# The dense layer's second pass: the gate row is formed in the first pass, and the scaled residual is added tile by tile

## The chip, the core and the metric

One core of a Trainium2 chip runs the whole program. Its engines each work through their own list of instructions in order: TensorE (PE in the profile; PEld are its weight loads), VectorE (DVE), ScalarE (ACT), GpSimd (POOL), and SyncE (SP), whose list here is a queue of transfers (SPq). The engines wait for each other by semaphores. The metric is the device time of one execution in microseconds. Before the change three runs gave 3324.81, 3330.18 and 3332.77 us; the median is 3330.18 us.

## The reference

The kernel computes a trunk of two layers on a sequence of 1024 tokens with 1024 channels. Each layer has a token mixer and a channel mixer; the channel mixer of layer 0 is a dense SwiGLU with 2816 hidden channels, that of layer 1 a mixture of eight experts. The change touches the dense one:

```python
def _dense_swiglu(u, w_gate, w_up, w_down):
    h = jax.nn.silu(jnp.einsum("bsd,df->bsf", u, w_gate)) * jnp.einsum("bsd,df->bsf", u, w_up)
    return jnp.einsum("bsf,fd->bsd", h, w_down)
...
    u = x * (1.0 + sc2) + sh2
    ff = _dense_swiglu(u, ffn_w_gate[j], ffn_w_up[j], ffn_w_down[j])
    x = _layernorm(DEEPNORM_ALPHA * x + (1.0 + g2) * ff, ln2_g[layer], ln2_b[layer])
```

`g2` is a row of 1024 numbers that comes from the conditioning vector. `x` in the last line is the output of the mixer's layer norm, so that `DEEPNORM_ALPHA * x` is a normalized tile times a scaled row of gains plus a scaled row of biases.

## The kernel before

Matrix products are made of three products in a reduced fp32 type: each operand is split into a high part (ScalarE, L352) and a low part (VectorE or GpSimd, L353), and `mm3` (L356 to L360) multiplies high by high, high by low and low by high into one PSUM bank of 128x512.

The dense layer has two passes. `dense_up` goes over eleven pairs of hidden tiles; for each pair it loads 256 columns of both up-projections, makes seven block products of each, and writes the pair's activation `h` to a DRAM buffer `hd` (L970). After each pair a hook issues some of the loads and VectorE work of the conditioning vector.

`dense_down` goes over the 22 hidden tiles in groups of two (nine groups) and four (the last). For a group it loads the activations `hf` from `hd` (L991) and splits them into `hh` (ScalarE) and `hl` (VectorE); it loads the down weights of two tiles in one transfer of 1 MB, `fd` (L997), multiplies them by the gate row `G` on GpSimd (L999), and splits them into `fdw..h` (ScalarE) and `fdw..l` (VectorE). Then, for each of eight token tiles and both halves of the 1024 output columns, it makes one PSUM bank: two hidden tiles times three products are six matmuls of 128x512. A group of two tiles so has 16 banks and 96 matmuls. VectorE adds each bank to the tile's running sum `xres` in SBUF (L1016). Six PSUM banks are in turn for this; a seventh bank can be started when the first has been added.

The running sums start as the residual: in group 0, before the first bank of a token tile, `residual` (L980 to L984) loads the normalized tile from DRAM and scales it in place with `gain` (L828 to L835): times the gain row `ln_g`, plus the bias row `ln_b`, the left half of the columns on GpSimd and the right half on VectorE. The two rows are loaded by `rows` (L815 to L826) and scaled on GpSimd (L824).

The gate row `G` is formed by `gate_row` (L325 to L337), which `dense_down` calls first (L977): for each of eight blocks VectorE makes a diagonal tile `dg` (L334), TensorE multiplies it by a tile of ones into a PSUM bank `gr` (L335), and VectorE adds one (L336).

The order on each engine isn't the order of the code: a scheduler places the instructions of the whole program by their dependences, by free buffers and by its own model of times. The buffers that matter here: two for the raw weights `fd`, six for the split weights `fdw`, 32 tiles of 128x1024 for `hf`, `hh`, `hl` and `xres`, six PSUM banks for `fd`.

Of the kernel before, what the change touches and what calls it, by code (L numbers as in the profile page):

```python
# [6 lines left out]
F32 = mybir.dt.float32  # L7
# [3 lines left out]
AF = mybir.ActivationFunctionType  # L11
OP = mybir.AluOpType
# [3 lines left out]
P = 128  # L16
D = 1024
# [50 lines left out]
class Trunk:  # L68
# [766 lines left out]
                eng.tensor_tensor(x[:, sl], x[:, sl], rows[i][:, sl], op=op)  # L835


    def dense_up(self, first, second, blocks, hook=lambda i: None):

# [114 lines left out]
        for fp in range(NF // 2):  # L956
            h = [self.s4([P, S], F32, f"h{2 * fp + j}") for j in range(2)]
            ms = [Matrix(fp, up, h) for up in range(2)]
            rest = (1, 6, 2, 7, 5, 4, 3)
            if fp == 0:  # L960
                for p in (1, 2):
                    for m in ms:
                        m.product(p)
                sums()
                rest = (6, 7, 5, 4, 3)
            for m in ms:
                for p in rest:
                    m.product(p)
            for j in range(2):
                nc.sync.dma_start(hd[(2 * fp + j) * P:(2 * fp + j + 1) * P, :], h[j])  # L970
            hook(fp)
        return hd

    def dense_down(self, l, hd, res_dram, rows, done, hook=lambda i: None):
        nc, w = self.nc, self.w
        dv = w["ffn_w_down"][0].rearrange("(f p) n -> p f n", p=P)
        G = self.gate_row(l, 5)  # L977
        xres = []

        def residual(t):  # L980
            x = self.s4([P, D], F32, f"xres{t}")
            nc.sync.dma_start(x, res_dram[t * P:(t + 1) * P, :])
            self.gain(x, rows, True)
            xres.append(x)  # L984
        groups = [2] * 9 + [4]
        f0 = 0
        for gi, gn in enumerate(groups):
# [16 lines left out]
                        self.split(*wd[-1], draw[:, j])  # L1004
            last = gi == len(groups) - 1
            for t in range(NT):
                if gi == 0:
                    residual(t)
                for dh in range(2):
                    ps = self.bank(f"fd{gi}{t}{dh}")  # L1010
                    for j in range(gn):
                        hk = [hs[j][x][:, t * P:(t + 1) * P] for x in range(2)]
                        self.mm3(ps, hk, [wd[j][x][:, dh * 512:(dh + 1) * 512] for x in range(2)],
                                 j == 0, j == gn - 1)
                    xs = xres[t][:, dh * 512:(dh + 1) * 512]
                    nc.vector.tensor_tensor(xs, xs, ps, op=OP.add)  # L1016
                if last:
                    self.normalize(xres[t], f"d{t}")
                    if t % 2 == 1:
                        done((t - 1, t), xres[t - 1:t + 1])  # L1020
            f0 += gn
            hook(gi)

    def residual_halves(self, pool, src, dst):
# [448 lines left out]
    def residual(self, xn, dst):  # L1473

        rows = self.rows(1, 1, pool=self.s4)

        def f(t):
            x = self.s4([P, D], F32, f"rx{t}")
            sl = slice(t * P, (t + 1) * P)
            self.nc.sync.dma_start(x, xn[sl, :])  # L1480
            self.gain(x, rows)
            self.nc.gpsimd.dma_start(dst[sl, :], x)
        return f
# [106 lines left out]
def build(tc, out, **w):  # L1590
    nc = tc.nc
    with ExitStack() as es:
# [5 lines left out]
        def ada_hook(n):  # L1598
            def f(*a):
                for _ in range(n):  # L1600
                    if todo:
                        T.ada_dve(*todo.pop(0))
            return f
# [29 lines left out]
            for t, x in zip(ts, tiles):  # L1633
                nc.sync.dma_start(st2["xr"][t * P:(t + 1) * P, :], x)
        T.results_init()
        hd = T.dense_up(*plain, blocks, lambda i: ada_hook(1 + i % 2)())
        T.dense_down(0, hd, xr, T.rows(0, 1, pool=lambda s, d, n: T.ln(n)), done2, ada_hook(1))
        npool.close()
        ada_hook(24)()
        T.ada_stack.close()  # L1640
# [42 lines left out]
```

## Time and profile before

| what | value |
|---|---|
| median of three runs | 3330.18 us |
| the profiled execution | 3329.88 us |
| its span | 3328.2 us |
| mean granted TensorE clock | 0.975 |
| PE busy | 3194.7 us, 96% |
| DVE busy | 2033.9 us, 61% |
| ACT busy | 1288.3 us, 39% |
| POOL busy | 706.2 us, 21% |
| second pass, group 0 begins | 927.68 us |
| group 1 begins | 982.73 us |
| group 2 begins | 1004.49 us |

The span is the profiled execution on the core; some 1.7 us of the measured time lie around it. Busy times are of the engine's own instructions. PE is near its limit over the program, so that what matters is where it isn't: its idle stretches, and stretches at the lower granted clock. The clock is given as a share of full speed: 1.00 is 2.4 GHz, 0.50 is 1.2 GHz, and a number between them is a mean over a stretch that has both.

### The profile page before, as it was taken

What the parts mean: (1) busy time and instruction counts of PE and PEld (TensorE: products, weight loads), DVE (VectorE), ACT (ScalarE), POOL (GpSimd) and SP (SyncE); (2) the same over time, 40 slices, a digit from 0 to 9 for tenths busy, and PEclk for the clock granted to TensorE, in tenths of its full rate; (3) what the DMA queues carried; (4) which work ended last, traced back from release to release, by engine and by line L of the source; (5) the groups of instructions that cost most, each with busy time, mean ns of one, the idle gap of its engine ahead of it and who ended that gap; (6) DMA issues with size and microseconds to landing.
All of it is one profiled execution on the core that took longest, in us unless ns stands there. A gap on an engine that the chain in (4) does not pass through costs nothing. (4 is left out here: it accounts for less than half of the span.)

```text
span 3328.2 us, 47451 instructions
## 1 busy us (share of the span) xinstructions
PE 3194.7 (96%) x18688; PEld 2841.8 (85%) x18688; DVE 2033.9 (61%) x2983; ACT 1288.3 (39%) x1991; POOL 706.2 (21%) x501
## 2 busy tenths in 40 slices
PE   8999988999969999999889999999999999999988
PEld 7878776888858889888789999999999998888876
DVE  6898887444487563455444366454554546666797
ACT  4322233333312143222143444444444455555563
POOL 2000108666672214101100042000000000000152
PEclk8999998999979999999889999999999999999998
DMA  8545631222243133121155476555655656566885
GB/s 249 161 150 162 233 115 64 84 94 76 97 178 106 46 128 98 55 84 57 46 177 158 152 237 227 175 176 167 196 189 185 192 176 204 190 202 209 272 284 181
DMA packets 429334, 518.48 MB, mean 156 GB/s; under 512 B 20969, under 2 KB 372461, under 8 KB 429104
## 3 DMA queue, kind: packets, MB, share of 16 engines
q1 hardware_dynamic: 414968, 468.32, 43.7%
q0 software_dynamic: 13840, 46.95, 3.9%
q8 instruction: 149, 2.44, 0.3%
q14 instruction: 81, 0.66, 0.1%
q10 hardware_dynamic: 296, 0.10, 0.0%
HBM read 459.37 MB, written 56.17 MB: 155 GB/s over the span
## 5 line engine op out<-in xcount | busy, mean ns | idle before, releaser
L1016 DVE TENSOR_TENSOR xres<-xres,fd 128x512 f32<-128x512 f32 x160 | 105.1, 684 | 68.1 <-PE fd L360 67.7
L1271 POOL DMA_INDIRECT xg<-xn,ixc x21 | 25.8, 1229 | 539.4 <-DVE ixc L1265 239.4
L307 DVE SCALAR_TENSOR_TENSOR acc<-ag,cond,acc 128x256 f32<-128x256 f32 x240 | 110.8, 506 | 40.1 <-DMA ag<-in_ada_w_dram 39.6
L927 DVE TENSOR_TENSOR fxu<-fu,fxu 128x512 f32<-128x512 f32 x77 | 52.2, 689 | 99.0 <-PE fu L360 98.9
L927 DVE TENSOR_TENSOR fxg<-fg,fxg 128x512 f32<-128x512 f32 x77 | 52.1, 689 | 97.7 <-PE fg L360 97.2
L1348 DVE TENSOR_TENSOR es<-es,eu 128x328 f32<-128x328 f32 (+4 forms) x110 | 49.1, 446 | 87.5 <-PE eu L360 86.0
L1416 POOL DMA_DIRECT2D ys<-yr x15 | 8.6, 573 | 439.5 <-ACT yr L1413 435.6
L999 POOL TENSOR_TENSOR fd<-fd,G 128x1024 f32<-128x1024 f32 x22 | 55.3, 2537 | 136.3 <-DMA fd<-in_ffn_w_down_dram 85.3
L952 POOL TENSOR_TENSOR h<-h,fxu 128x512 f32<-128x512 f32 x44 | 72.5, 1656 | 20.9 <-DVE fxu L927 20.5
L360 PE MATMUL L0mix<-L0woh,L0yl 128*128 128x512 f32 x128 | 51.1, 399 | 3.4 <-DVE L0yl L353 3.4
L358 PE MATMUL L0mix<-L0woh,L0yh 128*128 128x512 f32 x128 | 51.4, 402 | 1.7 <-ACT L0yh L352 1.5
L358 PE MATMUL L1mix<-L1woh,L1yh 128*128 128x512 f32 x128 | 52.7, 412 | 0.0
L359 PE MATMUL L0mix<-L0wol,L0yh 128*128 128x512 f32 x128 | 50.7, 396 | 1.5 <-DVE L0wol L353 1.5
L359 PE MATMUL L1mix<-L1wol,L1yh 128*128 128x512 f32 x128 | 52.0, 406 | 0.0
L360 PE MATMUL L1mix<-L1woh,L1yl 128*128 128x512 f32 x128 | 52.0, 406 | 0.0
L1291 PE MATMUL xt<-cst,xg 128*128 128x128 f32 (+2 forms) x168 | 30.9, 276 | 21.7 <-DMA xg<-xn,ixc 21.0
L1291 PEld LDWEIGHTS xt<-cst,xg 128*128 128x128 f32 (+2 forms) x168 | 22.5, 146 | 29.2 <-ACT ew001h L352 18.5
L352 ACT ACTIVATE hh<-hf 128x1024 fp32r<-128x1024 f32 x22 | 22.8, 1055 | 55.4 <-DMA hf<-hd 46.0
L1293 ACT ACTIVATE xu<-xt,B,A 128x256 f32<-128x256 f32 (+5 forms) x64 | 34.8, 572 | 21.2 <-PE xt L1291 18.5
L1347 ACT ACTIVATE es<-eg 128x328 f32<-128x328 f32 (+4 forms) x110 | 42.5, 387 | 0.0
L708 DVE RECIPROCAL L1rs<-L1rs 128x512 f32<-128x512 f32 x8 | 26.8, 3353 | 24.9 <-ACT L1rs L707 24.9
L504 POOL MEMSET L0z<- 128x2 f32 x4 | 0.5, 123 | 189.8 <-DVE L0yt L522 189.8
(6385 smaller groups left out, 12663.5 us busy)
## 6 DMA issues: line engine op xcount, KB each, us to landing
er<-in_moe_w_gate_dram SPq DMA_DIRECT2D x86, 1024.0 KB
er<-in_moe_w_up_dram SPq DMA_DIRECT2D x86, 1024.0 KB
dr<-in_moe_w_down_dram SPq DMA_DIRECT2D x70, 1024.0 KB
ag<-in_ada_w_dram SPq DMA_DIRECT2D x160, 256.0 KB
dr<-in_moe_w_down_dram SPq DMA_DIRECT2D x20, 768.0 KB
fg<-in_ffn_w_gate_dram SPq DMA_DIRECT2D x11, 1024.0 KB
fu<-in_ffn_w_up_dram SPq DMA_DIRECT2D x11, 1024.0 KB
hd<-h SPq DMA_DIRECT2D x22, 512.0 KB
```

The source lines that it names most:

```text
L307: V.scalar_tensor_tensor(acc, raw[:, kk], c, acc, op0=OP.mult, op1=OP.add)
L358: mm(out, a[0], b[0], start=start, stop=False)
L359: mm(out, a[0], b[1], start=False, stop=False)
L360: mm(out, a[1], b[0], start=False, stop=stop)
L927: add = lambda out, t: V.tensor_tensor(out, ps, t, op=OP.add)
L952: Q.tensor_tensor(d, d, c, op=OP.mult)
L999: nc.gpsimd.tensor_tensor(draw[:, j], draw[:, j], G, op=OP.mult)
L1016: nc.vector.tensor_tensor(xs, xs, ps, op=OP.add)
L1291: nc.tensor.transpose(ps[:, c * P:c * P + n], t[:n, k * P:(k + 1) * P], self.ident[:n, :n])
L1293: nc.scalar.activation(u, ps[:, :N], AF.Identity, bias=B[:, k:k + 1], scale=A[:, k:k + 1])
L1347: nc.scalar.activation(sg, pss[0][:, :N], AF.Silu)
L1348: nc.vector.tensor_tensor(sg, sg, pss[1][:, :N], op=OP.mult)
```

## The change

The call of `gate_row` moves from the start of `dense_down` to `dense_up`, after the seventh pair (`fp == 6`), inside `issue_after(put.ins)`, which queues those instructions of its block that are on the engine of the named one (here SP's queue, for the pair's last put) behind it; the instructions of `gate_row` are on VectorE and TensorE. The running sums get their buffers ahead of the groups. In group 0 they are not added to but written: ScalarE copies each PSUM bank to `xres`. The residual of token tile `gi` is loaded to another tile `xr` and scaled after group `gi`, over the whole width on GpSimd, and VectorE adds it to `xres` in one instruction of 128x1024.

```diff
-    def dense_up(self, first, second, blocks, hook=lambda i: None):
+    def dense_up(self, l, first, second, blocks, hook=lambda i: None):
...
             for j in range(2):
-                nc.sync.dma_start(hd[(2 * fp + j) * P:(2 * fp + j + 1) * P, :], h[j])
+                put = nc.sync.dma_start(hd[(2 * fp + j) * P:(2 * fp + j + 1) * P, :], h[j])
+            if fp == 6:
+                with self.tc.issue_after(put.ins):
+                    G = self.gate_row(l, 5)
             hook(fp)
-        return hd
-
-    def dense_down(self, l, hd, res_dram, rows, done, hook=lambda i: None):
+        return hd, G
+
+    def dense_down(self, l, hd, G, res_dram, rows, done, hook=lambda i: None):
...
-        G = self.gate_row(l, 5)
-        xres = []
+        xres = [self.s4([P, D], F32, f"xres{t}") for t in range(NT)]
 
         def residual(t):
-            x = self.s4([P, D], F32, f"xres{t}")
+            x = self.s4([P, D], F32, f"xr{t}")
             nc.sync.dma_start(x, res_dram[t * P:(t + 1) * P, :])
-            self.gain(x, rows, True)
-            xres.append(x)
+            self.gain(x, rows)
+            nc.vector.tensor_tensor(xres[t], xres[t], x, op=OP.add)
...
             for t in range(NT):
-                if gi == 0:
-                    residual(t)
                 for dh in range(2):
...
                     xs = xres[t][:, dh * 512:(dh + 1) * 512]
-                    nc.vector.tensor_tensor(xs, xs, ps, op=OP.add)
+                    if gi == 0:
+                        nc.scalar.activation(xs, ps, AF.Copy)
+                    else:
+                        nc.vector.tensor_tensor(xs, xs, ps, op=OP.add)
...
             f0 += gn
+            if gi < NT:
+                residual(gi)
             hook(gi)
```

The following rows are pieces of the engines' lists in both kernels (line, operation, output<-inputs, shape; the number behind a name is the buffer's).

TensorE, where the gate row's products stand. The tiles `u23tp` are the last transposes ahead of the dense layer, `gr` is the gate row's bank, `fg06`, `fg07` and `fg05` are products 6, 7 and 5 of the first pair. Before:

```order
L397 MATMUL u23tp3_3692<-cst_84,L0r7_3529 128x128
L335 MATMUL gr050_7185<-dg050_7186,cst_84 128x128
L335 MATMUL gr050_7185<-dg051_7189,cst_84 128x128
L335 MATMUL gr050_7185<-dg052_7192,cst_84 128x128
L335 MATMUL gr050_7185<-dg053_7195,cst_84 128x128
L335 MATMUL gr051_7199<-dg054_7200,cst_84 128x128
L335 MATMUL gr051_7199<-dg055_7203,cst_84 128x128
L358 MATMUL fg06_3893<-S2h0_3813,wg0T2_3890 128x512
L359 MATMUL fg06_3893<-S2l0_3814,wg0T2_3890 128x512
L358 MATMUL fg07_3910<-S3h0_3836,wg0T3_3907 128x512
L359 MATMUL fg07_3910<-S3l0_3837,wg0T3_3907 128x512
L335 MATMUL gr051_7199<-dg056_7206,cst_84 128x128
```

and now:

```order
L397 MATMUL u23tp3_3692<-cst_84,L0r7_3529 128x128
L335 MATMUL gr050_5923<-dg050_5924,cst_84 128x128
L335 MATMUL gr050_5923<-dg051_5927,cst_84 128x128
L335 MATMUL gr050_5923<-dg052_5930,cst_84 128x128
L335 MATMUL gr050_5923<-dg053_5933,cst_84 128x128
L335 MATMUL gr051_5937<-dg054_5938,cst_84 128x128
L335 MATMUL gr051_5937<-dg055_5941,cst_84 128x128
L358 MATMUL fg06_3893<-S2h0_3813,wg0T2_3890 128x512
L359 MATMUL fg06_3893<-S2l0_3814,wg0T2_3890 128x512
L358 MATMUL fg07_3910<-S3h0_3836,wg0T3_3907 128x512
L359 MATMUL fg07_3910<-S3l0_3837,wg0T3_3907 128x512
L335 MATMUL gr051_5937<-dg056_5944,cst_84 128x128
```

The rows are the same but for the buffers' numbers: all eight products of the gate row stand at the first pair in both lists. The diagonal tiles on VectorE stand at the same places in both lists too.

ScalarE in the second pass. `hh2` to `hh9` are the activations of hidden tiles 2 to 9, `fdw2h` the weights of tile 2, and `xres` is written by the copies of group 0, of which there are sixteen. Before:

```order
L352 ACTIVATE fdw1h_7233<-fd0_7225 128x1024
L352 ACTIVATE hh2_7436<-hf2_7435 128x1024
L352 ACTIVATE hh3_7442<-hf3_7441 128x1024
L352 ACTIVATE hh4_7609<-hf4_7608 128x1024
L352 ACTIVATE fdw2h_7450<-fd2_7447 128x1024
L352 ACTIVATE hh5_7615<-hf5_7614 128x1024
L352 ACTIVATE hh6_7782<-hf6_7781 128x1024
L352 ACTIVATE hh7_7788<-hf7_7787 128x1024
L352 ACTIVATE hh8_7965<-hf8_7964 128x1024
L352 ACTIVATE fdw3h_7455<-fd2_7447 128x1024
L352 ACTIVATE fdw4h_7623<-fd4_7620 128x1024
L352 ACTIVATE hh9_7971<-hf9_7970 128x1024
```

and now, from the last four copies:

```order
L1017 ACTIVATE xres6_7219<-fd061_7349 128x512
L1017 ACTIVATE xres7_7220<-fd070_7357 128x512
L352 ACTIVATE fdw3h_7420<-fd2_7412 128x1024
L1017 ACTIVATE xres7_7220<-fd071_7365 128x512
L352 ACTIVATE fdw4h_7593<-fd4_7590 128x1024
L352 ACTIVATE hh2_7401<-hf2_7400 128x1024
L352 ACTIVATE hh3_7407<-hf3_7406 128x1024
L352 ACTIVATE hh4_7579<-hf4_7578 128x1024
L352 ACTIVATE hh5_7585<-hf5_7584 128x1024
L352 ACTIVATE hh6_7757<-hf6_7756 128x1024
```

`fdw2h` now stands ahead of all sixteen copies, `fdw3h` ahead of the last of them, and `hh2` to `hh7` behind them; before, `hh2`, `hh3`, `hh4` stood ahead of `fdw2h` and `hh5` to `hh8` ahead of `fdw3h`.

SyncE's list of transfers in the second pass. `fd2`, `fd4`, `fd6` are the raw weights of groups 1, 2 and 3, `hf` the activations, `hd<-h20` and `hd<-h21` the last two activations on their way to DRAM. Before:

```order
L997 DMA fd4_7620<-in_ffn_w_down_dram 128x2x1024
L970 DMA hd_3729<-h20_6875 128x1024
L991 DMA hf3_7441<-hd_3729 128x1024
L970 DMA hd_3729<-h21_6876 128x1024
L991 DMA hf4_7608<-hd_3729 128x1024
L991 DMA hf5_7614<-hd_3729 128x1024
L991 DMA hf6_7781<-hd_3729 128x1024
L991 DMA hf7_7787<-hd_3729 128x1024
L991 DMA hf8_7964<-hd_3729 128x1024
L991 DMA hf9_7970<-hd_3729 128x1024
L991 DMA hf10_8138<-hd_3729 128x1024
L997 DMA fd6_7793<-in_ffn_w_down_dram 128x2x1024
```

and now:

```order
L993 DMA hf1_7227<-hd_3729 128x1024
L999 DMA fd2_7412<-in_ffn_w_down_dram 128x2x1024
L822 DMA ln1_g0_7207<-in_ln1_g_dram 128x1024
L822 DMA ln1_b0_7210<-in_ln1_b_dram 128x1024
L999 DMA fd4_7590<-in_ffn_w_down_dram 128x2x1024
L970 DMA hd_3729<-h20_6904 128x1024
L970 DMA hd_3729<-h21_6905 128x1024
L984 DMA xr0_7373<-xr0_2972 128x1024
L993 DMA hf2_7400<-hd_3729 128x1024
L999 DMA fd6_7768<-in_ffn_w_down_dram 128x2x1024
L993 DMA hf3_7406<-hd_3729 128x1024
L984 DMA xr1_7552<-xr0_2972 128x1024
```

The eight loads of the residual no longer stand ahead of `hf2` and `fd2`; one load of `xr` stands in each group. `fd2` now follows `hf1`, `hf2` has moved behind the last two activations, and `hf3` stands behind `fd6`, which it preceded by nine transfers.

On GpSimd the sixteen half-width operations of `gain` (L835) become sixteen of 128x1024; the product of `fd2` and `G` stands ahead of the scaling of the two rows; `xr0` stands behind the product of `fd4` and `G`, `xr1`, `xr2`, `xr3` behind that of `fd6`, and so on in pairs. On VectorE the sixteen operations of `gain` and the sixteen adds of group 0 are gone, and the eight adds of `xr` (L986 of the new code) stand one in each of groups 1 to 8, that of `xr0` ahead of group 1's first bank, that of `xr1` behind its seventh. TensorE's order in group 0 is the same; in group 1 the first six banks get their products with tile 2 first, and then those with tile 3.

## Rows read from the trace of the kernel before

**Rows 1.** The windows of the span around the second pass's first groups: start and end of the stretch, its length, then busy time (and instructions) of PE, PEld, DVE, ACT and POOL, the granted clock, the share of DMA, GB/s.

```profile
920.00:930.00 10.00, 10.00 (x46) 8.29 (x45) 5.40 (x7) 0.84 (x1) 6.20 (x3) 1.00 1.02 401
930.00:940.00 10.00, 6.00 (x27) 4.64 (x25) 10.00 (x9) 2.12 (x2) 10.00 (x7) 0.96 1.02 381
940.00:950.00 10.00, 0.00 (x0) 0.00 (x0) 10.00 (x7) 1.06 (x1) 10.00 (x7) 0.50 0.46 186
950.00:960.00 10.00, 2.71 (x6) 2.16 (x7) 9.95 (x7) 4.84 (x5) 10.00 (x5) 0.50 0.00 0
960.00:970.00 10.00, 7.36 (x25) 5.28 (x23) 9.67 (x6) 0.00 (x0) 10.00 (x5) 0.84 0.14 53
970.00:980.00 10.00, 8.44 (x20) 6.15 (x20) 6.04 (x8) 0.00 (x0) 4.75 (x4) 0.50 0.17 54
1000.00:1200.00 200.00, 200.00 (x898) 165.46 (x897) 133.70 (x196) 39.57 (x54) 35.26 (x17) 1.00 0.22 76
```

**Rows 2.** The timeline of PE from the start of group 0 (first row) to the starts of groups 1, 2 and 3 (last three rows): start, length as modelled, engine, line, operation, output<-inputs, and in brackets the idle time before it and what ended it.

```profile
927.68 0.39 PE L358 MATMUL fd<-fdw0h,hh 128*128 128x512 f32 x1
...
935.61 0.39 PE L360 MATMUL fd<-fdw1h,hl 128*128 128x512 f32 x1
957.29 0.80 PE L358 MATMUL fd<-fdw0h,hh 128*128 128x512 f32 x1 [21.29 <-DVE xres L1016]
...
972.25 0.63 PE L358 MATMUL fd<-fdw1h,hh 128*128 128x512 f32 x1
972.68 0.63 PE L359 MATMUL fd<-fdw1l,hh 128*128 128x512 f32 x1
...
982.73 0.39 PE L358 MATMUL fd<-fdw2h,hh 128*128 128x512 f32 x1
...
1004.49 0.39 PE L358 MATMUL fd<-fdw4h,hh 128*128 128x512 f32 x1
...
1026.25 0.39 PE L358 MATMUL fd<-fdw6h,hh 128*128 128x512 f32 x1
```

**Rows 3.** The groups of instructions from 927 to 1005 us, shapes kept apart: count, then busy time and mean ns of one.

```profile
L1016 DVE TENSOR_TENSOR xres<-xres,fd 128x512 f32<-128x512 f32 x31 | 20.0, 681 | 7.8 <-PE fd L360 7.6
L999 POOL TENSOR_TENSOR fd<-fd,G 128x1024 f32<-128x1024 f32 x6 | 17.2, 2882 | 15.5 <-DMA fd<-in_ffn_w_down_dram 15.5
L835 DVE TENSOR_TENSOR xres<-xres,ln_b 128x512 f32<-128x512 f32 x8 | 15.6, 2019 | 0.0
L835 POOL TENSOR_TENSOR xres<-xres,ln_b 128x512 f32<-128x512 f32 x8 | 14.3, 1822 | 0.0
L835 POOL TENSOR_TENSOR xres<-xres,ln_g 128x512 f32<-128x512 f32 x8 | 13.9, 1775 | 0.0
L835 DVE TENSOR_TENSOR xres<-xres,ln_g 128x512 f32<-128x512 f32 x8 | 10.1, 1328 | 0.2 <-POOL ln_g L824 0.2
```

**Rows 4.** The timeline of DVE in and after group 0: the scaling, one `hl`, the first adds, and two `hl`, of which the first lies beside GpSimd's work and the second doesn't.

```profile
928.81 10.09 DVE L835 TENSOR_TENSOR xres<-xres,ln_g 128x512 f32<-128x512 f32 x8 [0.24 <-POOL ln_g L824]
938.83 2.28 DVE L353 TENSOR_TENSOR hl<-hf,hh 128x1024 fp32r<-128x1024 f32 x1
941.03 15.61 DVE L835 TENSOR_TENSOR xres<-xres,ln_b 128x512 f32<-128x512 f32 x8
956.56 1.87 DVE L1016 TENSOR_TENSOR xres<-xres,fd 128x512 f32<-128x512 f32 x3
...
965.43 2.28 DVE L353 TENSOR_TENSOR hl<-hf,hh 128x1024 fp32r<-128x1024 f32 x1
967.63 0.67 DVE L1016 TENSOR_TENSOR xres<-xres,fd 128x512 f32<-128x512 f32 x1
...
977.90 1.22 DVE L353 TENSOR_TENSOR hl<-hf,hh 128x1024 fp32r<-128x1024 f32 x1
```

**Rows 5.** The timeline of ACT: a copy of a PSUM bank in the first pass, the waits for `fdw3h`, and two `hh`.

```profile
911.56 0.60 ACT L929 ACTIVATE fxu<-fu 128x512 f32<-128x512 f32 x1 [1.36 <-PE fu L360]
...
982.06 1.06 ACT L352 ACTIVATE fdw3h<-fd 128x1024 fp32r<-128x1024 f32 x1 [25.54 <-issue]
983.03 1.04 ACT L352 ACTIVATE fdw4h<-fd 128x1024 fp32r<-128x1024 f32 x1
983.98 1.99 ACT L352 ACTIVATE hh<-hf 128x1024 fp32r<-128x1024 f32 x2
992.17 1.06 ACT L352 ACTIVATE hh<-hf 128x1024 fp32r<-128x1024 f32 x1 [6.20 <-DMA hf<-hd]
```

**Rows 6.** The timeline of SP's queue at `fd6` and the first `hf` behind it (start and the time that the issues took).

```profile
985.38 0.38 SPq L997 DMA_DIRECT2D fd<-in_ffn_w_down_dram  x1
985.88 11.32 SPq L991 DMA_DIRECT2D hf<-hd  x3
```

**Rows 7.** The timeline of PE where it restarts after a gap in the last expert, and the windows of the granted clock there (columns as in rows 1).

```profile
3244.41 0.79 PE L1333 MATMUL eg<-xs,ew7210l 128*128 128x256 f32 x2 [2.31 <-DVE ew7210l L353]
...
3244.00:3247.00 3.00, 2.59 (x9) 2.30 (x10) 3.00 (x6) 1.70 (x3) 2.69 (x2) 0.50 0.74 217
3247.00:3250.00 3.00, 3.00 (x10) 2.52 (x10) 3.00 (x6) 1.57 (x3) 1.02 (x2) 0.50 1.06 404
3250.00:3253.00 3.00, 3.00 (x18) 2.61 (x18) 3.00 (x7) 1.27 (x4) 0.00 (x0) 1.00 0.98 315
```

**Rows 8.** The gate row at the first pair, 487 to 524 us: the groups of its instructions on DVE and PE, and the window of that stretch.

```profile
L334 DVE TENSOR_SCALAR dg<-cst,mod 128x128 f32<-128x128 f32 x7 | 6.4, 911 | 0.0
L335 PE MATMUL gr<-dg,cst 128*128 128x128 f32 x16 | 5.4, 449 | 18.6 <-DVE dg L334 18.3 <-ACT u L401 0.3
L336 DVE TENSOR_SCALAR G<-gr 128x512 f32<-128x512 f32 x1 | 0.7, 678 | 0.0
...
487.00:524.00 37.00, 15.02 (x47) 9.90 (x46) 36.32 (x33) 18.84 (x35) 28.30 (x19) 0.58 0.00 0
```

More of the change, by code (lines that the diff above doesn't have):

```diff
@@ L1635, in build @@
         T.results_init()
-        hd = T.dense_up(*plain, blocks, lambda i: ada_hook(1 + i % 2)())
-        T.dense_down(0, hd, xr, T.rows(0, 1, pool=lambda s, d, n: T.ln(n)), done2, ada_hook(1))
+        hd, Gd = T.dense_up(0, *plain, blocks, lambda i: ada_hook(1 + i % 2)())
+        T.dense_down(0, hd, Gd, xr, T.rows(0, 1, pool=lambda s, d, n: T.ln(n)), done2, ada_hook(1))
         npool.close()
```

## The prediction

> **What bounds the kernel now.** I read the page's busy shares first: PE is busy 96% of the span, so a gain has to come from its idle time or its slow clock. The windows then say where that is at the second pass. PE is full and at clock 1.00 in 920 to 930 and from 1000 on; between them it does 6.00, 0.00, 2.71, 7.36 and 8.44 us of work in five stretches of 10 us, much of it at clock 0.50, while DVE is busy 10.00, 10.00, 9.95 and 9.67 us of the first four [rows 1]. The timeline of PE names the wait: group 0 begins at 927.68, its sixth bank's last matmul starts at 935.61, and then PE waits 21.29 us for DVE's add to `xres` [rows 2]. It stops after six banks because there are six; the first one isn't free until DVE has added it. DVE can't, because it first scales the right halves of eight residual tiles, 10.09 us from 928.81 and 15.61 us from 941.03; its first add begins at 956.56 [rows 4].
>
> The price of the whole stall: group 0 takes 982.73 - 927.68 = 55.05 us. Group 1 takes 1004.49 - 982.73 = 21.76 us, group 2 the same [rows 2]; that is 96 matmuls at 0.2267 us. So 55.05 - 21.76 = 33.29 us is what a perfect group 0 would win, and the ceiling for this part of the change. No stretch from 1000 to 1200 has any to give: PE is busy 200.00 of 200 us there [rows 1].
>
> **The change part by part, the gate row.** The lists show that it isn't moved: its eight products and its diagonal tiles stand at the first pair in both. The block is tied to a put on SP, and nothing of the gate row is on SP, so the tie holds nothing back. The idle time there, 18.6 us ahead of its products [rows 8], stays. Value 0.
>
> **Group 0.** The copy of a bank on ACT took 0.60 us in the first pass [rows 5]; PE makes a bank in 6 x 0.2267 = 1.36 us. ACT has nothing else between the copies but `fdw3h`, 1.06 us [rows 5], with five banks in reserve. So group 0 should run unbroken, 927.68 + 21.76 = 949.44.
>
> **The step from group 0 to group 1.** This is where I expect some of it back. There are six buffers of split weights, so `fdw3h` and `fdw4h` must wait for PE to finish with `fdw0h` and `fdw1h`; before, this showed as `fdw3h` starting at 982.06, just ahead of the end of group 0 [rows 2, 5]. ACT now has `hh2` behind these two in its list. `fdw3h` starts when the last bank has used `fdw0h`, about 948.8, ends 949.8; the last copy ends near 950.3; `fdw4h` takes 1.04 us, of which the pipelined spacing is 0.97 (982.06 to 983.03) [rows 5]; `hh2` another 1.0. So `hh2` is there near 952.3, and PE restarts 952.3 - 949.4 = 2.9 us late.
>
> Then a transfer. `fd6` needs the raw buffer of `fd2`, which is free when DVE has made `fdw3l`: after 949.8 plus 1.2 us, near 951.1. `hf3` stands behind `fd6` on SP and is issued near 951.6. In the trace before, the same pair was issued at 985.38 and 985.88, and the `hh` of that `hf` began at 992.17 [rows 5, 6], 6.3 us after the issue. That gives `hh3` from 957.9 to 959.0. PE has 18 matmuls of group 1 that need only hidden tile 2, 18 x 0.2267 = 4.1 us, until 956.4; then it waits for `hh3` until 959.0, another 2.6 us. At half clock, with 0.43 us a matmul (972.25 to 972.68 [rows 2]), the 18 take 7.7 us, until 960.0, and the transfer is hidden; either way the remaining 78 matmuls begin near 959.3.
>
> 78 x 0.2267 = 17.7 us, so group 1 would end at 977.0 at full clock. The clock is not free: after the gap that ended at 957.29 it was 0.50 in 950 to 960 and on average 0.84 in 960 to 970, which is 3.2 us more at 0.50 [rows 1, 2], so about 5.9 us in all; after a gap of only 2.31 us at 3244.41 it was 0.50 for 5.6 us, to 3250 [rows 7]. Five to six us at half clock cost half of that, 2.5 to 3; I take 2.5, which gives 979.5. Bounds: 0 if the clock holds, and 78 x (0.43 - 0.2267) = 15.9 us if it stays low through group 1.
>
> **DVE in group 1.** It has 16 adds of 0.68 [rows 3], five `hl` and two adds of `xr`. A `hl` took 2.28 us beside GpSimd's work and 1.22 without; an add with its second input in PSUM took 0.67 beside it [rows 4]. The new add of 128x1024 has two inputs in SBUF as `hl` has, so I price it as `hl`: 1.2 to 2.3. GpSimd is busy for long there: `fd6` times `G`, two of 2.9 us [rows 3], and six operations for `xr1` to `xr3`, 1.8 us (half the width [rows 3]) to 2.9 us (this width) each. So DVE has at most 16 x 0.68 + 7 x 2.3 = 27 us of work against PE's 17.7 + 4.1. The six banks and the 24 matmuls with which group 2 begins before it needs `fdw5l`, 5.4 us, absorb most; I charge 2 us (bounds 0 and 5, the difference). Group 1 ends near 981.5, against 1004.49: 23 us won.
>
> **After that** nothing should be given back. Until group 8 DVE does one more add a group, 2.3 us at most, and DVE was busy 133.70 of 200 us there, 14.5 of 21.76 us a group [rows 1]. GpSimd gets two operations a tile, at most 5.8 us, beside 5.8 us of weights, out of 21.76. SP has a load of 0.5 MB more in each group beside 2 MB. The 16 half-width operations of DVE, 25.7 us, and its 16 adds in group 0 are gone; what hid them was nothing, which is why this pays. Cost 0, bounds 0 and 3 us.
>
> Sum: -33.3 (stall) + 2.9 + 2.6 (two gaps, or the slow clock in place of the second) + 2.5 (clock) + 2 (DVE) = -23.3 us. I take -23. From the profiled 3329.88 us that is 3306.9; the median 3330.18 stands 0.3 us above it, so I say 3307.
>
> **A rule of the Trainium skill against the trace.** The row first: `hl` takes 2.28 us beside a busy GpSimd and 1.22 us alone [rows 4], with two SBUF inputs; the add from PSUM isn't slowed. The Trainium skill (page "SBUF — State Buffer", section "Who interferes with whom") says that VectorE with two SBUF inputs and GpSimd reading SBUF exclude each other: the one that comes second is blocked until the other's instruction is over, without sharing. By the rule a `hl` or an `xr` add could wait for a whole GpSimd operation of 128x1024, now twice as wide as before. With 2.9 us on top of 1.2 the seven of group 1 would be 7 x 4.1 + 10.9 = 40 us of DVE's work, 13 us more than above, and the gain would be near 10. The trace shows a slowing to under twice the time, so I keep 2.3.
>
> **The rivals.** (a) The clock stays low through group 1, 15.9 instead of 2.5 us: the gain is 10 us, 3320. For it: PE ran at 0.50 in all of 970 to 980 although it was busy 8.44 us of them [rows 1]. Against it: after 957.29 it came back within 6 us.
>
> (a2) DVE's operations with two SBUF inputs wait for whole GpSimd operations, seven of them 4.1 us each in group 1: 40 us of DVE's list between 959 and PE's need of `fdw5l`, 13 us more than above, so again 10 us won, 3320. For it: `hl` nearly doubles beside GpSimd. Against it: it doesn't more than double [rows 4]. (This is what the Trainium skill's rule, named above, would make of it.)
>
> (b) The gate row moves after all. DVE is busy 36.32 of 37 us at the first pair [rows 8], so PE would wait for the operand sums instead; the gain is bounded by DVE's own six diagonal tiles and one add, 7 x 0.9 = 6.4 us: 3300.5. Against it: the lists.
>
> (c) No change, 3330: the residual isn't what PE waits for, but `hf` or weights, as ACT's `fdw3h` at 982.06 might suggest. Against it: PE's own wait names `xres`, and DVE's list leaves no doubt why.
>
> (d) Slower: the in-order adds of `xr`. DVE's add for tile k waits for a load on SP, which stands behind `fd` and `hf` loads that wait for buffers, and then for two GpSimd operations; the bank adds behind it wait too. Six banks are 8.2 us of reserve; each wait above that stops PE, and a stop of 2 us brings 2.5 us of slow clock. Seven such waits (`xr1` to `xr7`) with 3 us beyond the reserve make 7 x 5.5 = 38 us, 15 more than is won: 3345. It decides from 8.2 + 0.8 = 9 us of lateness per tile on. For it: the adds stand in the middle of the groups. Against it: GpSimd has 10 us of slack a group, and the loads stand a group ahead.
>
> **How the numbers follow.** Forecast -23 with 15 to 29 us won: 0.72. (a) 0.08, (a2) 0.05, (b) 0.03, (c) 0.06, (d) 0.06. What can be told from no change here is 0.2%, 6.7 us. The forecast, (a), (a2) and (b) are faster: 0.88; same 0.06; slower 0.06. The forecast's own range is 3301 to 3315; with (a) and (a2) at the one end and (b) at the other 80% lie in 3299 to 3321.
>
> **What would show it.** Group 0 unbroken from about 927.7 to 949.5 at 1.00; sixteen ACT copies near 0.6 us; the first matmul of `fdw2h` near 952 and of `fdw3h` near 959; the start of group 2 near 981.5; the `gr` products still at 490 to 520 with their idle time. The forecast is wrong if PE shows waits for DVE's `xres` above 2 us in groups 2 to 8, if group 1 takes over 35 us, or if the windows of 490 to 520 have changed.

## The result, and the profile after

The changed kernel takes 3306.94 us, the median of four runs (3305.16 to 3308.99); the kernel before, measured beside it, took 3328.97 us (four runs, 3324.81 to 3332.77). The ratio is 0.9936, with a 95% interval of 0.9924 to 0.9949. The ratio and its interval are computed from the single runs, here and below, and the ratio isn't the quotient of the two medians. The change is 22 us, where 23 were forecast. The profiled execution has a span of 3306.9 us.

The windows of the changed kernel; columns as in [rows 1]:

```profile
487.00:524.00 37.00, 15.03 (x51) 9.98 (x50) 34.50 (x32) 19.21 (x35) 26.48 (x17) 0.60 0.00 0
...
930.00:940.00 10.00, 10.00 (x46) 8.29 (x45) 2.63 (x2) 3.96 (x7) 10.00 (x7) 1.00 0.55 210
940.00:950.00 10.00, 10.00 (x46) 8.29 (x45) 0.00 (x0) 4.41 (x8) 6.66 (x3) 1.00 0.25 92
950.00:960.00 10.00, 7.33 (x26) 5.54 (x25) 4.72 (x4) 4.35 (x6) 1.59 (x1) 0.83 0.54 208
960.00:970.00 10.00, 9.81 (x44) 7.73 (x43) 7.22 (x7) 4.90 (x5) 9.92 (x5) 1.00 0.93 370
970.00:980.00 10.00, 8.58 (x38) 6.79 (x37) 10.00 (x11) 0.37 (x1) 9.84 (x4) 1.00 0.00 0
...
1000.00:1200.00 200.00, 195.56 (x886) 160.21 (x885) 147.86 (x205) 54.13 (x82) 54.57 (x26) 1.00 0.29 99
```

The stall of [rows 1] is gone: PE is full from 930 to 950, where DVE is busy for 2.63 of 20 us. The first row is that of [rows 8], with PE at 15.03 us of 37 as it was at 15.02. The last row says what the forecast had not: PE was busy 200.00 of 200 us there [rows 1], and is now idle for 4.44. Of these, 2.81 us are three waits for VectorE's `xres`, which follow; 1.50 us belong to transposes behind the second pass, which waited for 1.40 us before too, but then beyond 1200 us.

The timeline of PE gives the group borders (the first matmul of each even `fdw`) and every wait in groups 1 to 4:

```profile
929.91 0.39 PE L358 MATMUL fd<-fdw0h,hh 128*128 128x512 f32 x1
...
954.50 0.50 PE L358 MATMUL fd<-fdw2h,hh 128*128 128x512 f32 x1 [2.67 <-ACT hh L352]
...
956.38 0.63 PE L358 MATMUL fd<-fdw2h,hh 128*128 128x512 f32 x1
...
960.70 0.50 PE L358 MATMUL fd<-fdw3h,hh 128*128 128x512 f32 x1 [0.19 <-ACT hh L352]
...
977.43 0.50 PE L358 MATMUL fd<-fdw2h,hh 128*128 128x512 f32 x1 [1.42 <-DVE xres L1019]
...
980.30 0.39 PE L358 MATMUL fd<-fdw4h,hh 128*128 128x512 f32 x1
...
1002.23 0.39 PE L358 MATMUL fd<-fdw6h,hh 128*128 128x512 f32 x1
...
1004.87 0.50 PE L358 MATMUL fd<-fdw6h,hh 128*128 128x512 f32 x1 [0.44 <-DVE xres L1019]
...
1012.68 0.50 PE L358 MATMUL fd<-fdw6h,hh 128*128 128x512 f32 x1 [1.38 <-DVE xres L1019]
...
1026.46 0.39 PE L358 MATMUL fd<-fdw8h,hh 128*128 128x512 f32 x1
...
1036.20 0.50 PE L358 MATMUL fd<-fdw8h,hh 128*128 128x512 f32 x1 [0.99 <-DVE xres L1019]
...
1049.94 0.39 PE L358 MATMUL fd<-fdw10h,hh 128*128 128x512 f32 x1
```

Groups 0 to 4 take 24.59, 25.80, 21.93, 24.23 and 23.48 us, 120.03 together; before they took 55.05 + 4 x 21.76 = 142.09 [rows 2]. So 22.06 us were won in the second pass, and later groups take 21.76 in both. A whole execution is a poorer measure of it: group 0 began at 927.68 before and at 929.91 now, and in two more profiles of kernels with the same first pass at 926.75 and 930.16. The stall itself varies too: in the kernel with the gate row's half alone, whose lists are those of before, group 0 took 55.93 us. The experiments are therefore read by their group lengths first, and then by their times.

### The profile page after: what moved, and what is told of

It is laid out like the page before. It is cut to its first block, busy times and chain, and to the rows that moved or that the text cites. A ratio compares the mean times of both kernels' runs of the same rounds, so it can differ in the third digit from the quotient of the medians.

```text
span 3306.9 us, 47329 instructions
## 1 busy us (share of the span) xinstructions
PE 3189.4 (96%) x18688; PEld 2835.9 (86%) x18688; DVE 2014.5 (61%) x2959; ACT 1297.7 (39%) x2007; POOL 724.7 (22%) x501
## 5 line engine op out<-in xcount | busy, mean ns | idle before, releaser
L1019 DVE TENSOR_TENSOR xres<-xres,fd 128x512 f32<-128x512 f32 x144 | 93.0, 681 | 41.8 <-PE fd L360 41.7
```

## The experiments

The kernel before, the changed one and twelve experiments; the edits are to the second pass of the changed kernel unless said otherwise. Groups in us from the timeline of PE, taken as above.

| kernel | groups 0, 1, 2, 3, 4 | sum | median, us | ratio to before (95%) |
|---|---|---|---|---|
| before | 55.05, 21.76, 21.76, 21.76, 21.76 | 142.09 | 3328.97 | |
| changed | 24.59, 25.80, 21.93, 24.23, 23.48 | 120.03 | 3306.94 | 0.9936 (0.9924 to 0.9949) |
| changed, again | 24.59, 25.99, 21.89, 24.17, 23.49 | 120.13 | 3303.95 | 0.9942 (0.9927 to 0.9956) |
| gate row's half alone | 55.93, then 21.76 | 142.97 | 3327.43 | 0.9999 (0.9989 to 1.001) |
| gate row really moved | 24.58, 25.93, 23.17, 24.19, 23.62 | 121.49 | 3305.66 | 0.9943 (0.9925 to 0.9961) |
| all scaling on GpSimd, before's order | 60.88, then 21.76 | 147.92 | 3335.42 | 1.0031 (1.0018 to 1.0044) |
| group 0 copied by VectorE | 24.11, 26.76, 22.04, 24.20, 23.60 | 120.71 | 3306.48 | 0.9947 (0.9931 to 0.9964) |
| no scaling | 24.59, 23.99, 21.76, 21.76, 21.76 | 113.86 | not comparable | |
| scaling on VectorE | 24.59, 28.43, 21.76, 26.89, 21.76 | 123.43 | 3307.22 | 0.9947 (0.9930 to 0.9964) |
| scaling in halves | 24.59, 23.96, 23.23, 22.58, 23.12 | 117.48 | 3303.81 | 0.9928 (0.9912 to 0.9945) |
| bias row in group 0 | 24.11, 24.93, 21.76, 23.57, 23.15 | 117.52 | 3304.02 | 0.9925 (0.9910 to 0.9940) |
| step re-ordered | 23.55, 21.93, 24.21, 23.59, 23.97 | 117.25 | 3302.70 | 0.9924 (0.9909 to 0.9939) |
| bias row and step | 21.76, 22.43, 22.16, 22.35, 23.02 | 111.72 | 3300.22 | 0.9908 (0.9895 to 0.9922) |
| bias row, step, gate row | 21.76, 22.39, 24.57, 21.91, 23.28 | 113.91 | 3297.93 | 0.9920 (0.9904 to 0.9936) |

Each ratio is to the kernel before on the same chip, whose medians were 3322.41 to 3328.97 us on the chips that were used, so medians of different chips don't compare to within a few us.

### The gate row's half of the change alone

The kernel before, with its call of `gate_row` moved as in the change, and nothing else.

> The kernel before with the gate row's half of the change alone (the call after the seventh pair, tied to the put on SP). All theories that take the lists at their word: every engine's list is that of before, so no difference, ratio 0.999 to 1.001, and the gate row's products at 490 to 520 us. Rival (the tie does something that the lists don't show): the products later than 700 us, or a ratio below 0.998.

Ratio 0.9999, and the products began at 491.6 us. The tie to a transfer on SP moves nothing, and the whole gain is the residual's. That was read from the lists; this run shows it.

### The gate row really moved

```diff
-                add = lambda out, t: V.tensor_tensor(out, ps, t, op=OP.add)
+                def add(out, t):
+                    self.added = V.tensor_tensor(out, ps, t, op=OP.add)
...
-                with self.tc.issue_after(put.ins):
+                with self.tc.issue_after(self.added.ins):
                     G = self.gate_row(l, 5)
```

> The gate row really moved: its block is queued behind a VectorE add of the seventh pair, so that its eight diagonal tiles leave VectorE's list at the first pair. Theory (at the first pair VectorE's own list is the bound, 36 of 37 us busy): PE gets back only what VectorE spends on six diagonal tiles and one add, 5 to 6 us; the PE gaps there go from about 18.6 us ahead of the gate row's products to gaps of another name. Time about 3301 to 3303. Rival 1 (the gate row's products alone hold PE): the whole 18.6 us and its slow clock go, 3280 to 3290. Rival 2 (the place at the seventh pair costs as much, since the diagonal tiles then wait there): 3306 to 3308.

Tied to an instruction of VectorE, the products now stand at 780.9 to 796.8 us, behind that add and beside the eighth pair. At the first pair the timeline of PE shows what became of the waits:

```profile
508.82 0.79 PE L358 MATMUL fg<-S2h,wg0T 128*128 128x512 f32 x1 [16.78 <-ACT wg0T L352]
519.53 0.80 PE L360 MATMUL fg<-S2h,wg0T 128*128 128x512 f32 x1 [7.40 <-DVE wg0T L353]
```

The idle time in front of the gate row's products, 18.6 us [rows 8], now stands in front of the first products of the pair, for their split operands `wg0T`. From the last transpose to the second pair's first matmul it is 55.17 us, in the changed kernel 58.30: 3.1 us won. At the eighth pair the windows of this kernel (first row) and of the changed one show the same 24 us full of PE work, with eight more records in this one's, and the pair takes 40.01 instead of 38.08 us:

```profile
776.00:800.00 24.00, 24.00 (x115) 20.09 (x114) 16.76 (x25) 8.47 (x15) 11.71 (x9) 1.00 0.25 88
```

```profile
776.00:800.00 24.00, 24.00 (x107) 19.89 (x106) 11.21 (x14) 8.53 (x14) 14.18 (x11) 1.00 0.25 88
```

So 3.1 us won and 1.9 lost. Both theories had a part: the first on the small gain, rival 2 on the price at the new place, though that is no wait of the diagonal tiles but the products' own time, on an engine that had no hole for them. What is left, 1.2 us, is less than the time can tell; the median doesn't show it. And the five groups are 121.49 - 120.03 = 1.5 us longer, nearly all of it in group 2, which no term of the theory had: in sum the edit wins nothing that could be measured.

### All of the scaling on GpSimd, in the order of before

```diff
-            self.gain(x, rows, True)
+            self.gain(x, rows)
```

> The kernel before with the whole scaling of the residual tiles on GpSimd, still ahead of group 0's adds: VectorE's list has no scaling in it. Theory (what pays in the change is that group 0 doesn't wait for the scaled tiles at all): GpSimd needs 16 x 2.4 to 2.9 us and two pairs of weights, 50 to 57 us from 934 on, VectorE's adds wait for it, and group 0 takes 62 to 68 us in place of 55: 3336 to 3343, slower than before. Rival (VectorE's list alone held group 0): group 0 at 25 to 35 us, 3302 to 3312.

The waits of PE and the timeline of GpSimd in this kernel:

```profile
PE fd L358 <- DVE xres L1016: 36.6, 1, 36.6
```

```profile
934.54 23.39 POOL L835 TENSOR_TENSOR xres<-xres,ln_g 128x1024 f32<-128x1024 f32 x8
957.89 11.21 POOL L999 TENSOR_TENSOR fd<-fd,G 128x1024 f32<-128x1024 f32 x4
969.06 20.76 POOL L835 TENSOR_TENSOR xres<-xres,ln_b 128x1024 f32<-128x1024 f32 x8
```

Group 0 takes 60.88 us, a little under the 62 to 68 expected, and the kernel is 0.3% slower than before. Taking the scaling out of VectorE's list is not what pays by itself: as long as group 0's adds stand behind it, it matters which engine takes how long for it. That group 0 must do without the scaled tiles altogether isn't shown by this: before, all eight tiles are multiplied and then all eight get their bias row, ahead of the first add [rows 4], and an order tile by tile wasn't tried.

### Group 0 copied by VectorE

```diff
-                        nc.scalar.activation(xs, ps, AF.Copy)
+                        nc.vector.tensor_copy(xs, ps)
```

> The changed kernel with group 0's banks copied by VectorE in place of ScalarE. Theory (what stood in the way was the scaling in VectorE's list, not VectorE): VectorE has 19 us of idle time there, group 0 stays at 24.6 +- 1 us, 3305 to 3309. Rival (the engine that empties the banks matters): group 0 over 27 us, 3310 or more.

Group 0 at 24.11, all five 120.71: it doesn't matter, within 0.7 us, which engine empties the banks.

### No scaling, and the scaling on VectorE

```diff
-            self.gain(x, rows)
             nc.vector.tensor_tensor(xres[t], xres[t], x, op=OP.add)
```

> The changed kernel without the scaling of the residual tiles (the sixteen full-width operations on GpSimd are left out; the tiles are loaded and added unscaled). Theory (GpSimd's work beside it stretches VectorE's operations in groups 1 to 4, which is what PE waits for): hl and the adds of xr come back to 1.2 us outside of the weights' products, the waits of PE for xres in groups 1, 3 and 4 (1.42, 1.38, 0.99 us) go, groups 2, 3, 4 take 21.8 us each; 3301 to 3303. Rival (VectorE is late by its additional adds, whoever is beside it): groups 3 and 4 stay at 23.5 to 24.2 us, 3306.

```diff
-            self.gain(x, rows)
+            for row, op in zip(rows, (OP.mult, OP.add)):
+                nc.vector.tensor_tensor(x, x, row, op=op)
```

> The scaling of the residual tiles on VectorE in place of GpSimd: sixteen operations of 128x1024 more on VectorE, none on GpSimd. Theory (the stretching beside GpSimd costs more than the operations would): 2 x 1.2 us a tile on VectorE, 14.5 + 1.2 + 2.4 = 18.1 us of work in a group of 21.76, groups 2 to 4 at 21.8 to 22.5 us; 3302 to 3305. Rival (VectorE's load decides): groups 1 to 8 at 23 to 25 us, 3312 or more.

Without the scaling groups 2, 3 and 4 come to 21.76 us each and group 1 to 23.99: the adds of `xr` alone cost PE nothing in these groups, and GpSimd's scaling costs 120.03 - 113.86 = 6.2 us. It could have cost them in another way, by VectorE's adds standing in its list until the tile is scaled; but from 950 to 1050 us of the changed kernel VectorE waits for ScalarE and TensorE only, never for GpSimd's result. (The execution as a whole, 3448.40 us, isn't compared, since everything behind works on other numbers.) On VectorE the scaling costs more, 9.6 us, and it comes in two lumps, in groups 1 and 3. PE waits 2.47 and 2.12 us for `xres` there, and each time a stretch at half clock follows (0.51 in 967.8 to 971.1 and in 1015.6 to 1018.9). The theory was right on the cause and wrong on this remedy: the rival, VectorE's load, holds for groups 1 and 3, though not for 2 and 4, which are at 21.76.

### The scaling in halves

What VectorE and GpSimd do to each other is in their timelines. First VectorE's in the changed kernel, then GpSimd's beside it:

```profile
967.00 3.08 DVE L353 TENSOR_TENSOR hl<-hf,hh 128x1024 fp32r<-128x1024 f32 x1
...
971.20 2.22 DVE L986 TENSOR_TENSOR xres<-xres,xr 128x1024 f32<-128x1024 f32 x1
...
979.09 1.21 DVE L353 TENSOR_TENSOR hl<-hf,hh 128x1024 fp32r<-128x1024 f32 x1
...
1007.48 3.42 DVE L353 TENSOR_TENSOR fdw8l<-fd,fdw8h 128x1024 fp32r<-128x1024 f32 x1
```

```profile
944.47 2.40 POOL L835 TENSOR_TENSOR xr<-xr,ln_b 128x1024 f32<-128x1024 f32 x1
...
966.60 2.40 POOL L835 TENSOR_TENSOR xr<-xr,ln_b 128x1024 f32<-128x1024 f32 x1
968.95 3.39 POOL L835 TENSOR_TENSOR xr<-xr,ln_g 128x1024 f32<-128x1024 f32 x1
...
979.10 3.48 POOL L835 TENSOR_TENSOR xr<-xr,ln_b 128x1024 f32<-128x1024 f32 x1
...
1006.54 3.26 POOL L835 TENSOR_TENSOR xr<-xr,ln_b 128x1024 f32<-128x1024 f32 x1
```

Add start and length. The `hl` ends at 970.08, GpSimd's operation at 969.00. The add of `xr` ends at 973.42, GpSimd's at 972.34. `fdw8l` ends at 1010.90, GpSimd's at 1009.80. Each time VectorE is done 1.08 to 1.10 us after GpSimd, about what the operation takes by itself. By these ends it isn't slowed all along; it waits for GpSimd's operation to end, and then runs. In the third pair VectorE starts first, at 979.09, and is done in 1.21 us; GpSimd starts at 979.10 and takes 3.48 instead of the 2.40 of 944.47, by the same 1.08.

```diff
-            self.gain(x, rows)
+            for h in range(2):
+                sl = slice(h * 512, (h + 1) * 512)
+                for i, op in enumerate((OP.mult, OP.add)):
+                    nc.gpsimd.tensor_tensor(x[:, sl], x[:, sl], rows[i][:, sl], op=op)
```

> The changed kernel with GpSimd's scaling in halves: 32 operations of 128x512 in place of 16 of 128x1024, the same work. Theory (exclusion: an operation of VectorE with two SBUF inputs that comes while a GpSimd operation runs waits for that operation's end and then takes its own 1.1 us): beside the halves no such operation of VectorE takes over 2.6 us (in the changed kernel up to 3.1, and up to 3.44 beside the weights' products, which stay whole), each ends about 1.1 us after a GpSimd operation's end, and groups 1 to 4 take 1 to 3 us less than 95.4 us. Rival (the two engines share a bandwidth in proportion): the same lengthening in sum as before, groups 1 to 4 at 95 to 96 us, and no fixed distance between the ends. Time 3302 to 3306 by the one, 3304 to 3307 by the other.

The timeline of VectorE in this kernel:

```profile
965.56 2.06 DVE L353 TENSOR_TENSOR hl<-hf,hh 128x1024 fp32r<-128x1024 f32 x1
...
968.81 2.29 DVE L989 TENSOR_TENSOR xres<-xres,xr 128x1024 f32<-128x1024 f32 x1
...
982.53 2.30 DVE L353 TENSOR_TENSOR fdw6l<-fd,fdw6h 128x1024 fp32r<-128x1024 f32 x1
```

Beside the halves nothing takes over 2.31 us; beside the weights' products, still whole, the longest is 3.44. Groups 1 to 4 take 92.89 us in place of 95.44, 2.6 less for the same work in smaller pieces. All fourteen lengthened operations of VectorE there end 1.07 to 1.09 us after an operation of GpSimd; for the first two of the rows above these are

```profile
965.23 1.30 POOL L988 TENSOR_TENSOR xr<-xr,ln_b 128x512 f32<-128x512 f32 x1
...
968.74 1.27 POOL L988 TENSOR_TENSOR xr<-xr,ln_g 128x512 f32<-128x512 f32 x1
```

They end at 966.53 and 970.01, VectorE's at 967.62 and 971.10. This fixed distance is what speaks for the theory. The gain alone doesn't: in sum the fourteen are 13.2 us over their own 1.22 each, and the twelve of the changed kernel were 14.9, so that the rival's "same lengthening in sum" is nearly met.

### The bias row in group 0, the step, and both

```diff
-            self.gain(x, rows)
+            nc.gpsimd.tensor_tensor(x, x, rows[0], op=OP.mult)
...
-                        nc.scalar.activation(xs, ps, AF.Copy)
+                        nc.vector.tensor_tensor(xs, ps, rows[1][:, dh * 512:(dh + 1) * 512], op=OP.add)
```

> The changed kernel with half of GpSimd's scaling taken away without leaving anything out: VectorE, which idles in group 0, adds the bias row to each of group 0's banks in place of ScalarE's copy, so that GpSimd only multiplies by the gain row (eight operations of 128x1024 in place of sixteen). Theory (GpSimd's scaling beside VectorE costs the 4 us of groups 1 to 4): groups 1 to 4 together 2 to 4 us shorter than the 95.4 us of the changed kernel, 3303 to 3305. Rival (the number of SBUF adds on VectorE decides, which stays): groups 3 and 4 stay at 23.5 to 24.2 us, 3306 to 3307.

Groups 1 to 4 take 93.41 us, 2.0 less: the lower end of what was expected.

The step's edit queues a group's raw weights behind the `hf` of two groups earlier, and the second tile's weights behind the group's own `hh`:

```diff
-                nc.sync.dma_start(draw, dv[:, fb:fb + 2])
+                load = lambda: nc.sync.dma_start(draw, dv[:, fb:fb + 2])
+                if gi > 2:
+                    with self.tc.issue_after(puts[gi - 2].ins):
+                        load()
+                else:
+                    load()
...
+                        if j and gi:
+                            with self.tc.issue_after(high.ins):
+                                wd.append(self.wsplit(draw[:, j], f"fdw{fb + j}"))
```

> The changed kernel with the step from group 0 to group 1 re-ordered: the loads of hf2 and hf3 stand ahead of fd6 on SP, and hh2 and hh3 ahead of fdw3h on ScalarE, directly behind the last copy. Theory (the step's cost is the order on ScalarE and SP, 2.7 us of wait for hh2 and about 2 us of slow clock after it): hh2 about 1 us earlier, PE restarts 1.5 to 2 us after group 0's end, and if the clock holds the 18 matmuls take 4.1 us; groups 0 and 1 together 47 to 49 us in place of 50.4; 3303 to 3306. Rival (VectorE's backlog in group 1 sets its end anyway): 50 us for both, 3306 to 3307.

Groups 0 and 1 take 45.48 us, less than expected: PE's wait for `hh2` is 1.63 us instead of 2.67, the wait for `hh3` is gone, and the clock holds. Groups 2 to 4 give 2.1 us of it back (71.77 in place of 69.64): VectorE is busy 22.00 of 22 us from 974 to 996, and PE waits 1.71 us for `xres` in group 2. The rival was right on that much.

> Both of the last two edits: VectorE empties group 0 and adds the bias row there, ScalarE has hh2 and hh3 ready during group 0, and hf3 doesn't wait for fd6. If both theories hold, group 0 takes 21.8 to 22.3 us, group 1 22 to 23, groups 2 to 4 21.8 to 22.8: 7 to 9 us less than the changed kernel, 3298 to 3300. If only the scaling matters 3303 to 3305, if neither 3306.

With both, groups 0 to 4 take 111.72 us, 8.3 less than in the changed kernel and 2.9 over five perfect ones. The windows of this kernel at the step, columns as before:

```profile
940.00:950.00 10.00, 10.00 (x46) 8.29 (x45) 5.32 (x8) 2.12 (x2) 6.89 (x3) 1.00 0.68 258
950.00:955.00 5.00, 4.76 (x22) 3.60 (x20) 3.66 (x6) 2.96 (x3) 0.00 (x0) 1.00 0.00 0
955.00:960.00 5.00, 4.91 (x21) 4.05 (x22) 4.80 (x7) 0.00 (x0) 0.00 (x0) 1.00 0.26 81
960.00:970.00 10.00, 10.00 (x45) 8.26 (x44) 10.00 (x11) 3.18 (x3) 7.71 (x3) 1.00 0.94 379
```

The border between the groups is at 951.88 us. PE is full around it but for 0.33 us in 950 to 960, and the clock stays at 1.00.

### The changed kernel again, beside the best one

> The changed kernel itself, beside the next one on the same chip: 22 to 24 us below before; groups 0 to 4 take 120 us together.

> All three edits that won anything: the bias row added in group 0, the re-ordered step, and the gate row really moved. Theory (the wins add): groups 0 to 4 take 111 to 113 us in place of 120, the first pair 3 us less, the seventh 2 us more: 8 to 10 us below the changed kernel on the same chip. Rival (they share one cause, or the gate row's place costs more with the rest): within 5 us of the changed kernel.

On one chip the changed kernel takes 3303.95 us and the one with all three edits 3297.93, 6.0 us less; 8 to 10 had been expected. The five groups take 113.91 in place of 120.13 us, 6.2 less. Group 2 is at 24.57 where the kernel without the gate row's edit has 22.16; without the other two edits the gate row's made it longer as well, 23.17 against 21.93. Why wasn't tried. The kernel with bias row and step alone, at a ratio of 0.9908, is as good by what the intervals can tell; both are faster than the kernel before, and by their groups than the changed one.

## Why the prediction came out right, point by point

**The gate row, 0.** Right: it isn't moved, and the half alone measures 0.9999. The price of rival (b) was too high. It allowed 6.4 us; the first pair gave 3.1, and the products' 1.9 us at the new place had no term at all, because I looked for a wait of the diagonal tiles there and not at PE, which is full. The second pass took the rest.

**Group 0, 33.3 us to win.** Right. PE runs unbroken through it and the copies take 0.60 us each. That it wasn't enough to take the scaling off VectorE's list is shown by the kernel with all of it on GpSimd: still ahead of the adds, and slower than before.

**The step, 2.9 + 2.6.** The order was right. ScalarE's timeline in the changed kernel, and SP's:

```profile
951.01 1.06 ACT L352 ACTIVATE fdw3h<-fd 128x1024 fp32r<-128x1024 f32 x1
951.98 0.58 ACT L1017 ACTIVATE xres<-fd 128x512 f32<-128x512 f32 x1
952.45 1.05 ACT L352 ACTIVATE fdw4h<-fd 128x1024 fp32r<-128x1024 f32 x1
953.40 1.05 ACT L352 ACTIVATE hh<-hf 128x1024 fp32r<-128x1024 f32 x1
959.59 1.06 ACT L352 ACTIVATE hh<-hf 128x1024 fp32r<-128x1024 f32 x1 [5.14 <-DMA hf<-hd]
```

```profile
953.36 0.38 SPq L999 DMA_DIRECT2D fd<-in_ffn_w_down_dram  x1
953.83 0.42 SPq L993 DMA_DIRECT2D hf<-hd  x1
```

`fdw3h`, the last copy, `fdw4h`, `hh2`: PE waits 2.67 us for it, and group 0 with this is 2.83 over 21.76. `hf3` was there 5.8 us after its issue, not 6.3. Half clock stretched the 18 matmuls, so that the second gap shrank to 0.19 and both together took 960.70 - 954.50 = 6.2 us. That one hides the other is shown by the kernel with the gate row really moved, whose clock was at 1.00 there (954.0 to 961.0):

```profile
954.25 0.50 PE L358 MATMUL fd<-fdw2h,hh 128*128 128x512 f32 x1 [2.66 <-ACT hh L352]
...
960.59 0.50 PE L358 MATMUL fd<-fdw3h,hh 128*128 128x512 f32 x1 [1.96 <-ACT hh L352]
```

The gap is 1.96 there, and the stretch 6.34 us, no shorter than at half clock.

**The clock, 2.5.** Wrong, by counting twice. I had written that either the gap of 2.6 us or the slow clock hides the other, and then added a further 2.5 us for the clock in the 78 matmuls behind. There the clock was at 1.00 already. The two terms together measured 2.1 us (6.2 - 18 x 0.2267), not 5.1.

**VectorE in group 1, 2.** Right in size, but not by its working: the 78 matmuls took 980.30 - 960.70 = 19.6 us, 1.9 over 17.7, with 1.42 of it one wait for `xres`. The seven operations with two SBUF inputs, five `hl` and two adds of `xr`, took 13.0 us, where 7 x 2.3 = 16.1 had been charged. VectorE had less to do than I thought, and later: it was idle for 3.65 and 2.10 us ahead of 964 us.

**"After that nothing should be given back", 0 with a bound of 3.** This step failed. Groups 2 to 4 gave back 0.17 + 2.47 + 1.72 = 4.4 us, beyond the bound. The step charged one more add a group at 2.3 us and left VectorE's other work at what it had taken before, 14.5 us a group. It put at nothing, without saying why, that GpSimd's new scaling would lengthen `hl` and `fdw..l` too, as it had assumed for group 1. In groups 2 to 4 VectorE has twenty operations with two SBUF inputs; they took 34.75 us, 10.3 over 1.22 each. The three adds of `xr` are 2.6 of this, within what was charged; the seventeen `hl` and `fdw..l` are 7.7, and these had no term. VectorE had no slack left for them: it was busy 24.29 of 24.3 us from 1002.2 to 1026.5. Without the scaling the three groups take 21.76 each, which shows that the scaling is the cause. Over groups 1 to 4 twelve operations are longer than 1.3 us, 29.5 us in all; at 1.22 each they would be 14.6. The six banks covered most of these 15 us, not all.

**The rule of the Trainium skill.** The timelines side with it: whichever of the two engines comes second waits until the other's operation is over, and then takes its own time, 1.08 us here. The Trainium skill's page "SBUF — State Buffer", section "Who interferes with whom", says this. I had set it aside because 2.28 us looked like a slowing to under twice. The trace before already spoke for the rule. These are GpSimd's operations beside the two `hl` of 2.28 us in [rows 4]:

```profile
938.32 1.71 POOL L835 TENSOR_TENSOR xres<-xres,ln_g 128x512 f32<-128x512 f32 x1
...
964.38 2.25 POOL L835 TENSOR_TENSOR xres<-xres,ln_b 128x512 f32<-128x512 f32 x1
```

They end at 940.03 and 966.63; the `hl` end at 941.11 and 967.71, both 1.08 us later. The 2.28 was a wait for the rest of a half-width operation and then the `hl` itself. So the sharing that the forecast assumed was a misreading, and beside the full-width operations the same `hl` took 2.83 and 3.08, and `fdw8l` 3.42. The rival (a2) was nevertheless priced too high, at 13 us: its seven operations at 4.1 us would be 28.7, and they took 13.0. A wait lasts only for what is left of GpSimd's operation, and 15 of the 27 operations with two SBUF inputs in groups 1 to 4 weren't lengthened; the mean of all is 1.77 us, below the 2.3 that I kept.

**The signs.** The prediction called itself wrong if PE waited more than 2 us for `xres` in groups 2 to 8. No single wait there is above 1.38 us, but the three together are 2.81.

The errors, 3.0 us too much at the step and 4.4 too little after it, nearly cancel, which is why the sum of -23 met a measured -22. To that extent the number was luck. A sum that comes out is no proof of its terms.

## What to carry to other kernels

Where a residual must be added to an accumulation, start the sums from the product and add the prepared tile later: then no engine's preparation stands between PSUM and the next bank. Moving the preparation to another engine ahead of the same adds, in the same order, did not pay. Where VectorE and GpSimd run side by side on SBUF, price a VectorE operation with two SBUF inputs at its own time plus what is left of GpSimd's, and price so all of them that come beside GpSimd's new work, not only the new ones. Narrower operations on GpSimd shortened a wait (`fdw8l`: 2.31 us in place of 3.42). Work moved out of an idle stretch into a full one costs its whole time there.

## What the runs showed of the hardware

The wait between VectorE and GpSimd is exact: of twelve lengthened operations of VectorE in groups 1 to 4 of the changed kernel all ended 1.08 to 1.10 us after a GpSimd operation did, and adds with one input in PSUM kept their 0.68 us throughout (0.67 to 0.69). It goes both ways (3.48 us on GpSimd in place of 2.40).

A gap of 2.67 us in PE's work was followed by a stretch at 1.2 GHz from 955.5 to 958.9 (matmuls 0.43 us apart). Gaps of 2.18 and 2.19 us at the same place, in the kernels with VectorE's copies and with the bias row, were followed by one too (0.50 in 954.5 to 957.7, 0.54 in 955.6 to 958.8). After the gap of 1.63 us in the re-ordered kernel there was none, and group 1 took 21.93 us; but there was none either after the gap of 2.66 us in the kernel with the gate row really moved. So the length of the gap alone doesn't decide it, and what does isn't shown here.
